# Values of dilated attention computed in token order and reordered through device memory

## The chip, the cores and the metric

The kernel runs on one core of one Trainium2 chip. Its time is what the device needs for one execution, in microseconds (us). TensorE multiplies matrices, VectorE and ScalarE work element by element, GpSimd helps, and SyncE (SP in the rows) issues the transfers between the device's memory (DRAM) and the on-chip memory (SBUF). Each engine takes its instructions in the order of the program and waits for semaphores; matmuls write to PSUM.

## The reference

Two transformer blocks, one behind the other, over 1024 tokens of width 1024, in 32-bit floats. The change concerns the first block's attention. Its 12 heads stand in three groups of four, with dilations 1, 4 and 16: in a group with dilation d a token sees those tokens before it that lie a multiple of d away.

```
ATT_GROUPS = ((128, 1), (512, 4), (2048, 16))      # window, dilation

def _dilated_window_attention(q, k, v, dilation, n_steps, slopes):
    def to_sub(t):
        t = t.reshape(B, L, dilation, H, Dh).transpose(0, 2, 1, 3, 4).reshape(Z, L, H, Dh)
    ...
    qb = to_sub(q).reshape(Z, nb, BLK, H, Dh).astype(jnp.float32)
    kb = band(to_sub(k)).astype(jnp.float32)
    vb = band(to_sub(v)).astype(jnp.float32)
    s = jnp.einsum('znqhd,znkhd->znhqk', qb, kb) * (Dh ** -0.5)
    ...
    s = jnp.where(valid[None, :, None], s + bias[None, None], -jnp.inf)
    lse = jax.nn.logsumexp(s, axis=-1)
    p = jnp.exp(s - lse[..., None])
    o = jnp.einsum('znhqk,znkhd->znqhd', p, vb)

def first_block(x, ...):
    u = _rmsnorm(h, norm_mix_g[l])
    z = jnp.einsum('bsd,dn->bsn', u, w_in[l])
    q, k, v, pz, ga, gp = jnp.split(z, offs, axis=-1)
    a = _attention_branch(q, k, v).astype(dt)
    ...
```

`to_sub` is the dilated order: all tokens with the same remainder modulo d stand together.

## The kernel before

The activations lie transposed in SBUF: channels on the 128 partitions, the 1024 tokens along the row. Every 32-bit product is made of three matmuls of the type fp32r: each operand is split into a high and a low part (`uh`, `ul` for the activations, `whi`, `wlo` for the weights), and high times high, high times low and low times high are summed. The division by the norm of a token (`rstd`) is done after the matmul, at the eviction from PSUM.

The program is a list of jobs, run in order by `run`. A job is one slab of weights (a `Unit`, 512 KB) and the matmuls that use it. Ahead of each job `run` emits the split of the next job's weights (ScalarE for `whi`, line 337, VectorE for `wlo`, line 338) and the load of weights for later jobs (line 320, on SP's queue), as far as the three `raw` buffers go. Attention is not a job: it is a chain of small steps (`attn1`, a generator in a lane of `bg`), and `tick`, called after every few matmuls of a job, advances it by one. A step (one block of 128 queries and two heads) consists of the scores (line 722), the softmax (VectorE line 737, which adds the table `alibi`, and ScalarE line 742), the flip (line 752, transposes on TensorE, copied back by lines 754 and 755) and the values (line 768). The table is loaded by line 705 when the chain first advances, and the result goes to DRAM by line 781.

For each group g there are jobs for two halves of q, two halves of k, and then one V job (`v_job`, lines 667 to 686) with two units. The V job makes the values with tokens on the partitions: here the activations are the stationary operand, 128 tokens at a time, and the weights (256 columns) the moving one. There are 2 halves x 4 blocks of tokens x 8 chunks of channels x 3 parts = 192 matmuls, lines 680 to 682. The block of tokens is picked by `tok`, in the order of the group: consecutive tokens for g = 0, every 4th for g = 1, every 8th for g = 2 (dilation 16 is treated as 8 with a mask). Since tokens stand on the partitions, `rstd` is needed as a column per block of tokens: `rcols`, ahead of the V job of group 0, transposes it for all three groups, 24 transposes with 6 small copies out of PSUM into `rcol`. `v_store1` scales and evicts each half of the values (line 694), into tiles that `attn1` reads from SBUF.

After the V job of group 1 come pool jobs, q and k of group 2, more pool jobs, the V job of group 2, and then the jobs `grp_job` and `pool_out_job`. The second block has two V jobs of its own in token order; their store (`v_store2`, line 1549) already goes through DRAM, and `attn2` loads windows of it (line 1563).

Of the kernel before, what the change touches and what calls it, by code (L numbers as in the profile page):

```python
# [10 lines left out]
F32 = mybir.dt.float32  # L11
F32R = mybir.dt.float32r
AF = mybir.ActivationFunctionType
ALU = mybir.AluOpType

P = 128
T = 1024
# [6 lines left out]
DIL = (1, 4, 16)  # L24
# [36 lines left out]
class Unit:  # L61


    def __init__(self, name, k0, kc, c0, cw):
        self.name, self.k0, self.kc, self.c0, self.cw = name, k0, kc, c0, cw
        self.n = kc * cw
        self.off = None
        self.early = 2
        self.parts = [self]
        self.raw = self.hi = self.lo = None  # L70
# [126 lines left out]
class Kern:  # L197
    def __init__(self, tc, ins, out, es):
        self.tc, self.nc, self.ins, self.out = tc, tc.nc, ins, out
        nc = self.nc  # L200
        self.pc = es.enter_context(tc.tile_pool(name="pc", bufs=1))
        self.pw = es.enter_context(tc.tile_pool(name="pw", bufs=3))
        self.pz = es.enter_context(tc.tile_pool(name="pz", bufs=36))
        self.pd = es.enter_context(tc.tile_pool(name="pd", bufs=1, space=bass.MemoryType.DRAM))
        self.pm = es.enter_context(tc.tile_pool(name="pm", bufs=2, space=bass.MemoryType.PSUM))
        self.pb = es.enter_context(tc.tile_pool(name="pb", bufs=4, space=bass.MemoryType.PSUM))
        self.bg = [deque(), deque(), deque()]
        self.late = []
        self.hook_wait = 0
        self.credit = 0.0  # L210
        self.rate = 0.0
        self.hooks = []
        self.ph = None
        self.phs = None

        self.cst = self.pc.tile([P, NCST], F32, tag="cst", name="cst")
        self.ones = self.pc.tile([P, P], F32R, tag="ones", name="ones")
        self.gg = self.pc.tile([P, 8], F32, tag="gg", name="gg")
        self.rcol = self.pc.tile([P, 24], F32, tag="rcol", name="rcol")
        self.cpos = self.pc.tile([P, 16], F32, tag="cpos", name="cpos")  # L220
        self.cneg = self.pc.tile([P, 16], F32, tag="cneg", name="cneg")
        self.oscr = [self.pd.tile([T, 264], F32, tag=f"oscr{g}", name=f"oscr{g}") for g in range(3)]
        self.v2 = [self.pd.tile([T, 256], F32, tag=f"v2{i}", name=f"v2{i}") for i in range(2)]
        self.x1 = [self.pd.tile([P, T], F32, tag=f"x1{i}", name=f"x1{i}") for i in range(NC)]
        self.sgr = [self.pd.tile([P, T], F32, tag=f"sgr{i}", name=f"sgr{i}") for i in range(NC)]
        self.sg2 = [self.pd.tile([P, T], F32, tag=f"sg2{i}", name=f"sg2{i}") for i in range(NC)]
        self.res = [self.pd.tile([P, T], F32, tag=f"res{i}", name=f"res{i}") for i in range(NC)]
        self.ud = [self.pd.tile([P, T], F32, tag=f"ud{i}", name=f"ud{i}") for i in range(NC)]
        self.po = [self.pd.tile([P, T], F32, tag=f"po{i}", name=f"po{i}") for i in range(NC)]
        self.hidd = [self.pd.tile([P, 2, T], F32, tag=f"hid{i}", name=f"hid{i}") for i in range(N_HID // 2)]  # L230
        self.quart = {(w, b, dp): {q: Quarter(w, b, dp, q) for q in ((0, 0), (0, 1), (1, 0), (1, 1))}
                      for w in ("w_mlp_out", "w_ff2") for b in range(N_BLK + 1) for dp in range(2)}
        self.sums = {(*key, i): self.pd.tile([P, T], F32, tag="sums" + "_".join(map(str, (*key, i))), name="sums")
                     for key in self.quart for i in (5, 6, 3, 7)}
        self.to_sum = list(self.quart)
        self.op = []
        self.nraw = 0
        self.rec = [self.pd.tile([P, T], F32, tag=f"rec{i}", name=f"rec{i}") for i in range(NC)]
# [357 lines left out]
                nc.sync.dma_start(y, x)  # L596
            yield

    def rcols(self, groups):
        nc = self.nc  # L600
        for g in groups:
            d = DIL[g]
            for q in range(2):
                ps = self.bank()
                for j in range(4):
                    nc.tensor.transpose(ps[:, j * P:(j + 1) * P], self.tok(self.rstd, d, 4 * q + j), self.ident())
                nc.vector.tensor_copy(
                    self.rcol[:, 8 * g + 4 * q:8 * g + 4 * q + 4],
                    ps.rearrange("p (j t) -> p j t", j=4)[:, :, 0],
                )  # L610

    @staticmethod
    def tok(ap, d, j):


        if d == 1:
            return ap[:, j * P:(j + 1) * P]
        if d == 4:
            return ap.rearrange("p (i d) -> p d i", d=4)[:, j // 2, (j % 2) * P:(j % 2 + 1) * P]
        return ap.rearrange("p (i d) -> p d i", d=8)[:, j, :]  # L620


    def qk_job(self, un, dst, d, scale, key):
# [40 lines left out]
                self.evac(lambda t=t, ps=ps: self.scaled(t, ps, 0.125))  # L664
        return fn

    def v_job(self, uns, store, d, g):

        nc = self.nc

        def fn():
            for q in range(2):
                ps = self.mm()
                for j in range(4):
                    o = ps[:, j * 256:(j + 1) * 256]
                    for k in range(NC):
                        un, kk = uns[k // 4], k % 4
                        uh, ul = self.us[k]
                        th, tl = self.tok(uh, d, 4 * q + j), self.tok(ul, d, 4 * q + j)
                        nc.tensor.matmul(o, th, un.h(kk, 0, 256), start=(k == 0), stop=False)  # L680
                        nc.tensor.matmul(o, th, un.l(kk, 0, 256), start=False, stop=False)
                        nc.tensor.matmul(o, tl, un.h(kk, 0, 256), start=False, stop=(k == NC - 1))  # L682
                        if k % 2 == 1:
                            self.tick()
                store(q, ps)
        return fn

    def v_store1(self, dst, g):
        nc = self.nc

        def store(q, ps):
            t = self.z(nm="v")
            for j in range(4):
                nc.vector.tensor_scalar(
                    t[:, j * 256:(j + 1) * 256], ps[:, j * 256:(j + 1) * 256],
                    self.rcol[:, 8 * g + 4 * q + j:8 * g + 4 * q + j + 1], None, ALU.mult,
                )
            dst["v", q] = t
        return store

    def attn1(self, g, src):
        nc = self.nc
# [1168 lines left out]
    def program(self):  # L1871
# [9 lines left out]
        qkv = [dict() for _ in range(3)]  # L1881
# [7 lines left out]
        for g in range(3):  # L1889
            pr.rate = RATE_A[g]  # L1890
            uns = [Unit("w_in", 0, NC, 256 * g + P * c, P) for c in range(2)]
            if g == 0:
                self.first = uns
                pr.job([], self.first_job(qkv[g]), 1)
            else:
                for c, un in enumerate(uns):
                    pr.job([un], self.qk_job(un, qkv[g], DIL[g], 0.125, ("q", c)))
            for c in range(2):
                un = Unit("w_in", 0, NC, 768 + 256 * g + P * c, P)
                pr.job([un], self.qk_job(un, qkv[g], DIL[g], None, ("k", c)), 1 if (g, c) == (0, 0) else None)  # L1900
            uns = [Unit("w_in", 4 * i, 4, 1536 + 256 * g, 256) for i in range(2)]
            vf = self.v_job(uns, self.v_store1(qkv[g], g), DIL[g], g)

            def vfn(vf=vf, g=g):
                if g == 0:
                    self.rcols(range(3))
                    self.phase("phA")
                vf()
                self.bg[0].append(self.attn1(g, qkv[g]))
                if g == 2:  # L1910
                    self.bg[0].append(self.combine1())
            if g == 2:
                pool_jobs((2, 1, 0))
            pr.job(uns, vfn)
            if g == 1:
                pool_jobs((5, 4, 3))
# [61 lines left out]
        for hh in range(2):  # L1978
# [6 lines left out]
                pr.job([un], self.qk2_job(un, qkv2[hh], ("k", c), None, 4 + 2 * hh + c),  # L1985
                       1 if (hh, c) == (0, 0) else None)
            uns = [Unit("w_in_2", 4 * i, 4, 1024 + 256 * hh, 256) for i in range(2)]
            vf = self.v_job(uns, self.v_store2(hh), 1, 0)

            def vfn2(vf=vf, hh=hh):  # L1990
                if hh == 0:
                    self.rcols((0,))
                    self.phase("phB")
                    self.bv = self.ph.tile([P, 512], F32, tag="bv", name="bv")
                    self.nc.sync.dma_start(self.bv, self.ins["bv"])
                    self.lru_const()
                vf()
                self.bg[0].append(self.attn2(hh, qkv2[hh]))
# [241 lines left out]
```

## Time and profile before

| | |
|---|---|
| median of three runs | 3020.59 us (3020.18 to 3021.07) |
| the profiled execution, its own time | 3018.67 us |
| its span in the trace | 3016.7 us |
| TensorE busy | 97% of the span |
| VectorE, ScalarE, GpSimd busy | 63%, 39%, 37% |

Times inside the trace are counted from the start of the span. The busy share is a mean over stages with different limits; what a change is worth is read in the stage that it touches.

### The profile page before, as it was taken

To read this page: it belongs to the slowest core of one execution; us is meant where nothing else is said; L and a number is where in the kernel's file an instruction comes from. 1 tells how busy PE (TensorE), PEld (TensorE's weight loads), DVE (VectorE), ACT (ScalarE), POOL (GpSimd) and SP (SyncE) were. 2 spreads that over 40 slices of the span, in tenths; PEclk is the share of its full clock that TensorE was granted. 3 is DMA by queue.
4 is the path that set the end of the run, shared out by engine and by line. 5 is a ranking of instruction groups with operands and counts; after the bars stand their busy time and mean duration, and the time that the engine had idled before them with its cause. 6 is when DMAs were issued, how large, how long until landed. Compare 5 with 4: busy or idle time off the path is not lost. (4 is left out here: it accounts for less than half of the span.)

```text
span 3016.7 us, 35237 instructions
## 1 busy us (share of the span) xinstructions
PE 2922.4 (97%) x13438; PEld 2406.6 (80%) x13438; DVE 1901.6 (63%) x2329; ACT 1168.6 (39%) x1786; POOL 1115.5 (37%) x554
## 2 busy tenths in 40 slices
PE   9999999999989999999899999998899899999987
PEld 8898987888878888877778778886788788888866
DVE  6424345565675567899844446888555765577797
ACT  3312044222344454334323325545424344444334
POOL 0012101555254433386400005544154444443486
PEclk9999999999999999999999999999999999999999
DMA  4201125778323355442232311211577233354442
GB/s 154 80 29 54 33 68 178 271 270 294 112 86 110 112 202 168 153 154 84 95 110 84 104 65 62 91 60 67 220 282 259 81 111 110 108 199 166 151 160 84
DMA packets 136567, 398.15 MB, mean 132 GB/s; under 512 B 14032, under 2 KB 29520, under 8 KB 136400
## 3 DMA queue, kind: packets, MB, share of 16 engines
q1 hardware_dynamic: 136400, 395.91, 37.7%
q8 instruction: 106, 1.74, 0.2%
q14 instruction: 61, 0.50, 0.1%
HBM read 285.66 MB, written 110.20 MB: 131 GB/s over the span
## 5 line engine op out<-in xcount | busy, mean ns | idle before, releaser
L1112 PE MATMUL bk<-obl,whi 128*128 128x512 f32 x864 | 340.9, 395 | 14.1 <-DVE obl L477 14.1
L1112 PE MATMUL bk<-obh,wlo 128*128 128x512 f32 x864 | 339.9, 393 | 1.5 <-DVE wlo L477 1.5
L476 ACT ACTIVATE whi<-raw 128x512 fp32r<-128x512 f32 (+2 forms) x256 | 204.7, 808 | 351.7 <-PE bk L1112 316.6
L1112 PE MATMUL bk<-obh,whi 128*128 128x512 f32 x864 | 339.6, 393 | 1.2 <-ACT obh L476 0.8
L477 DVE TENSOR_TENSOR wlo<-raw,whi 128x512 fp32r<-128x512 f32 (+2 forms) x256 | 306.2, 1199 | 50.2 <-ACT whi L476 48.7
L438 PE MATMUL mm<-uh,whi 128*128 128x512 f32 x864 | 278.0, 403 | 8.2 <-DVE v L1544 6.7
L1112 PE MATMUL bk<-tt,whi 128*128 128x512 f32 x896 | 275.7, 389 | 0.0
L438 PE MATMUL mm<-ul,whi 128*128 128x512 f32 x864 | 269.8, 393 | 2.2 <-DVE ul L490 2.2
L438 PE MATMUL mm<-uh,wlo 128*128 128x512 f32 x864 | 268.6, 392 | 0.1
L377 POOL TENSOR_TENSOR wsum<-wsum 128x1024 f32<-128x1024 f32 x64 | 180.2, 2825 | 238.4 <-DMA wsum<-in_w 227.3
L338 DVE TENSOR_TENSOR wlo<-raw,whi 128x1024 fp32r<-128x1024 f32 (+3 forms) x140 | 216.4, 1551 | 34.2 <-ACT whi L337 34.1
L477 DVE TENSOR_TENSOR obl<-hraw,obh 128x1024 fp32r<-128x1024 f32 x112 | 192.8, 1721 | 28.4 <-ACT obh L476 25.2
L438 PEld LDWEIGHTS mm<-uh,whi 128*128 128x128 f32 x864 | 157.2, 189 | 66.1 <-issue 34.2
L1112 PEld LDWEIGHTS bk<-obl,whi 128*128 128x128 f32 x864 | 164.3, 190 | 52.9 <-DVE obl L477 18.6
L337 ACT ACTIVATE whi<-raw 128x1024 fp32r<-128x1024 f32 (+3 forms) x140 | 135.3, 974 | 160.3 <-PE mm L682 94.0
L1112 PEld LDWEIGHTS bk<-tt,whi 128*128 128x128 f32 x896 | 168.2, 188 | 34.9
L438 PEld LDWEIGHTS mm<-ul,whi 128*128 128x128 f32 x864 | 163.4, 189 | 39.0 <-DVE ul L490 4.0
L1112 PEld LDWEIGHTS bk<-obh,whi 128*128 128x128 f32 x864 | 164.2, 190 | 36.5 <-ACT obh L476 1.2
L1112 PEld LDWEIGHTS bk<-obh,wlo 128*128 128x128 f32 x864 | 164.2, 190 | 36.3 <-DVE wlo L477 2.3
L438 PEld LDWEIGHTS mm<-uh,wlo 128*128 128x128 f32 x864 | 163.3, 189 | 35.5 <-DVE wlo L338 0.5
L1112 PE MATMUL bk<-tt,wlo 128*128 128x512 f32 x448 | 174.3, 389 | 0.0
L1731 POOL TENSOR_SCALAR yt<-yt 128x1024 f32<-128x1024 f32 x8 | 16.8, 2096 | 411.0 <-DMA sgr<-sgr 303.6
(362 smaller groups left out, 6510.3 us busy)
## 6 DMA issues: line engine op xcount, KB each, us to landing
raw<-in_w SPq DMA_DIRECT2D x190, 512.0 KB
wsum<-in_w SPq DMA_DIRECT2D x64, 512.0 KB
sums<-wsum SPq DMA_DIRECT2D x64, 512.0 KB
hraw<-hid SPq DMA_DIRECT2D x64, 512.0 KB
raw<-sums SPq DMA_DIRECT2D x64, 512.0 KB
hid<-h SPq DMA_DIRECT2D x56, 512.0 KB
wraw<-in_w SPq DMA_DIRECT2D x28, 512.0 KB
rb<-in_rpb SPq DMA_DIRECT2D x24, 384.0 KB
```

What stands on the lines that cost most here:

```text
L337: nc.scalar.activation(un.hi, un.raw, AF.Copy)
L338: nc.vector.tensor_tensor(un.lo, un.raw, f32(un.hi), ALU.subtract)
L377: G.tensor_tensor(d, x, y, f)
L438: nc.tensor.matmul(dst[a], w, half(x, a), start=(i == 0 and q == 0), stop=(i == n - 1 and q == 2),)
L476: self.nc.scalar.activation(hi, src, AF.Copy)
L477: self.nc.vector.tensor_tensor(lo, src, f32(hi), ALU.subtract)
L1112: nc.tensor.matmul(ps, w[:, k * P:(k + 1) * P], x, start=(k == 0 and q == 0), stop=(k == n - 1 and q == 2))
L1731: G.tensor_scalar(t, t, 0.044715, 1.0, ALU.mult, ALU.add)
```

## The change

The V jobs of groups 1 and 2 take their tokens in natural order, as group 0 does; `tok` and its strided views are gone. The evicted halves are stored to a DRAM tile (`v1`, one for each of the two groups), two stores of 512 KB. After the second half, `v_load` reads them back in the order that the attention wants: four transfers of 256 KB for group 1 (rows of 1 KB, every 4th token), two of 512 KB for group 2 (four rows of 1 KB that lie together, for each partition). The column of reciprocal norms is needed in one order only: `rcols` makes 8 transposes and 2 copies.

```
-        self.rcol = self.pc.tile([P, 24], F32, tag="rcol", name="rcol")
+        self.rcol = self.pc.tile([P, 8], F32, tag="rcol", name="rcol")
...
+        self.v1 = [self.pd.tile([T, 256], F32, tag=f"v1{i}", name=f"v1{i}") for i in range(2)]
...
-    def rcols(self, groups):
-        nc = self.nc
-        for g in groups:
-            d = DIL[g]
-            for q in range(2):
-                ps = self.bank()
-                for j in range(4):
-                    nc.tensor.transpose(ps[:, j * P:(j + 1) * P], self.tok(self.rstd, d, 4 * q + j), self.ident())
-                nc.vector.tensor_copy(
-                    self.rcol[:, 8 * g + 4 * q:8 * g + 4 * q + 4],
-                    ps.rearrange("p (j t) -> p j t", j=4)[:, :, 0],
-                )
+    def rcols(self):
+        nc = self.nc
+        for q in range(2):
+            ps = self.bank()
+            for j in range(4):
+                t = (4 * q + j) * P
+                nc.tensor.transpose(ps[:, j * P:(j + 1) * P], self.rstd[:, t:t + P], self.ident())
+            nc.vector.tensor_copy(
+                self.rcol[:, 4 * q:4 * q + 4], ps.rearrange("p (j t) -> p j t", j=4)[:, :, 0])
...
-                        th, tl = self.tok(uh, d, 4 * q + j), self.tok(ul, d, 4 * q + j)
+                        th, tl = (x[:, (4 * q + j) * P:(4 * q + j + 1) * P] for x in (uh, ul))
...
     def v_store1(self, dst, g):
         nc = self.nc
+        d = DIL[g]
 
         def store(q, ps):
             t = self.z(nm="v")
             for j in range(4):
                 nc.vector.tensor_scalar(
                     t[:, j * 256:(j + 1) * 256], ps[:, j * 256:(j + 1) * 256],
-                    self.rcol[:, 8 * g + 4 * q + j:8 * g + 4 * q + j + 1], None, ALU.mult,
+                    self.rcol[:, 4 * q + j:4 * q + j + 1], None, ALU.mult,
                 )
-            dst["v", q] = t
+            if d == 1:
+                dst["v", q] = t
+                return
+            v = self.v1[g - 1]
+            nc.sync.dma_start(
+                v[512 * q:512 * q + 512, :].rearrange("(j p) c -> p j c", p=P),
+                t.rearrange("p (j c) -> p j c", j=4))
+            if q == 1:
+                for r in range(2):
+                    dst["v", r] = self.v_load(v, d, r)
         return store
+
+    def v_load(self, v, d, q):
+
+        t = self.z(nm="vd")
+        o = t.rearrange("p (j c) -> p j c", j=4)
+        if d == 4:
+            src = v.rearrange("(h p d) c -> d p h c", p=P, d=4)
+            for e in range(2):
+                self.nc.sync.dma_start(o[:, 2 * e:2 * e + 2], src[2 * q + e])
+        else:
+            self.nc.sync.dma_start(o, v.rearrange("(p j) c -> p j c", j=8)[:, 4 * q:4 * q + 4])
+        return t
...
             def vfn(vf=vf, g=g):
                 if g == 0:
-                    self.rcols(range(3))
+                    self.rcols()
```

## Rows read from the trace of the kernel before

**Rows 1.** The page: the span, and busy time by engine.
```profile
span 3016.7 us, 35237 instructions
...
PE 2922.4 (97%) x13438; PEld 2406.6 (80%) x13438; DVE 1901.6 (63%) x2329; ACT 1168.6 (39%) x1786; POOL 1115.5 (37%) x554
```

**Rows 2.** By stretch: length, busy PE, PEld, DVE, ACT, POOL, granted clock, DMA share, GB/s.
```profile
138.00:203.00 65.00, 65.00 (x338) 61.85 (x338) 15.87 (x50) 11.69 (x35) 0.00 (x0) 1.00 0.11 35
```

**Rows 3.** Timeline of TensorE: start, duration, instruction; V jobs of groups 0, 1, 2.
```profile
56.49 0.36 PE L680 MATMUL mm<-whi,uh 128*128 128x256 f32 x1
...
79.59 0.63 PE L438 MATMUL mm<-uh,whi 128*128 128x512 f32 x2
...
189.05 0.40 PE L680 MATMUL mm<-whi,uh 128*128 128x256 f32 x1
...
201.65 0.63 PE L438 MATMUL mm<-uh,whi 128*128 128x512 f32 x2
...
338.03 0.29 PE L680 MATMUL mm<-whi,uh 128*128 128x256 f32 x1
...
384.13 0.62 PE L438 MATMUL mm<-plh,whi 128*128 128x512 f32 x2
```

**Rows 4.** Line 680's weight loads: shortest, median, longest (ns), first and last start.
```profile
L680 PEld LDWEIGHTS mm<-whi,uh x320: 186/192/341, 56.5 to 1643.1; 128*128 128x128 f32 x160
```

**Rows 5.** Timeline of TensorE: the 24 transposes of `rcols`.
```profile
53.07 2.06 PE L606 MATMUL bk<-cst,rstd 128*128 128x128 f32 x16
55.58 1.16 PE L606 MATMUL bk<-cst,rstd 128*128 128x128 f32 x8 [0.45 <-DVE rcol L607]
```

**Rows 6.** Timeline of SP's queue: at group 1's V job, and in block two.
```profile
185.72 0.42 SPq L320 DMA_DIRECT2D raw<-in_w  x1
186.19 0.44 SPq L705 DMA_DIRECT2D alibi<-in_alibi  x1
...
1645.42 0.38 SPq L1549 DMA_DIRECT2D v<-v  x1
...
1648.79 0.32 SPq L1563 DMA_DIRECT2D vw<-v  x1
```

**Rows 7.** Timeline of all engines after the V jobs of groups 1 and 2.
```profile
201.85 1.66 DVE L694 TENSOR_SCALAR v<-mm,rcol 128x256 f32<-128x256 f32 x4 [16.57 <-PE mm L682]
...
205.01 0.29 DVE L737 CUSTOM_DVE_ANT_0 s<-bk,alibi 128x128 f32<-128x128 f32 x1 [0.36 <-PE bk L722]
...
213.85 0.38 PE L752 MATMUL bk<-cst,s 128*128 128x128 f32 x2
...
227.36 1.04 ACT L337 ACTIVATE whi<-raw 128x1024 fp32r<-128x1024 f32 x1
...
391.51 0.28 DVE L737 CUSTOM_DVE_ANT_0 s<-bk,alibi 128x128 f32<-128x128 f32 x1
...
392.39 0.71 PE L752 MATMUL bk<-cst,s 128*128 128x128 f32 x2
...
396.52 0.56 PE L768 MATMUL bk<-v,pt 128*128 128x64 f32 x4
```

**Rows 8.** A 512 KB load and its reader (timeline); transfers from 75 to 79 us.
```profile
506.15 0.42 SPq L943 DMA_DIRECT2D uraw<-ud  x1
...
509.76 1.06 ACT L476 ACTIVATE ubh<-uraw 128x1024 fp32r<-128x1024 f32 x1 [2.30 <-DMA uraw<-ud]
...
DMA packets 358, 1.33 MB, mean 333 GB/s; under 512 B 33, under 2 KB 33, under 8 KB 358
```

**Rows 9.** TensorE after idle time (in brackets); one stretch with its granted clock.
```profile
505.04 1.22 PE L438 MATMUL mm<-ath,whi 128*128 128x512 f32 x2 [4.25 <-ACT merged L956]
...
505.00:510.00 5.00, 4.96 (x12) 3.90 (x13) 2.39 (x4) 2.70 (x5) 0.00 (x0) 0.50 0.57 174
...
2131.95 1.22 PE L438 MATMUL mm<-ah,whi 128*128 128x512 f32 x2 [2.71 <-DVE mixed L1843]
...
2148.51 0.73 PE L438 MATMUL mm<-ah,whi 128*128 128x512 f32 x2 [1.86 <-DVE mixed L1843]
```

More of the change, by code (lines that the diff above doesn't have):

```diff
@@ L597, in keep_x1 @@
             yield
-    def rcols(self, groups):
+    def rcols(self):
         nc = self.nc
-        for g in groups:
-            d = DIL[g]
-            for q in range(2):
-                ps = self.bank()
-                for j in range(4):
-                    nc.tensor.transpose(ps[:, j * P:(j + 1) * P], self.tok(self.rstd, d, 4 * q + j), self.ident())
-                nc.vector.tensor_copy(
-                    self.rcol[:, 8 * g + 4 * q:8 * g + 4 * q + 4],
-                    ps.rearrange("p (j t) -> p j t", j=4)[:, :, 0],
-                )
[L612 to L620, printed above, removed]
+        for q in range(2):
[5 more added lines that the diff above has]
+                self.rcol[:, 4 * q:4 * q + 4], ps.rearrange("p (j t) -> p j t", j=4)[:, :, 0])
     def qk_job(self, un, dst, d, scale, key):
@@ L665, in first_job, with v_job @@
         return fn
-    def v_job(self, uns, store, d, g):
+    def v_job(self, uns, store):
         nc = self.nc
@@ L1901, in program @@
             uns = [Unit("w_in", 4 * i, 4, 1536 + 256 * g, 256) for i in range(2)]
-            vf = self.v_job(uns, self.v_store1(qkv[g], g), DIL[g], g)
+            vf = self.v_job(uns, self.v_store1(qkv[g], g))
             def vfn(vf=vf, g=g):
                 if g == 0:
-                    self.rcols(range(3))
+                    self.rcols()
                     self.phase("phA")
@@ L1987, in program @@
             uns = [Unit("w_in_2", 4 * i, 4, 1024 + 256 * hh, 256) for i in range(2)]
-            vf = self.v_job(uns, self.v_store2(hh), 1, 0)
+            vf = self.v_job(uns, self.v_store2(hh))
             def vfn2(vf=vf, hh=hh):
                 if hh == 0:
-                    self.rcols((0,))
+                    self.rcols()
                     self.phase("phB")
```

## Prediction

> **What bounds the kernel now.** I read the page first: the span is 3016.7 us and TensorE is busy for 97% of it [rows 1]. The reader should see a kernel whose length is the sum of its matmuls, so that a change is worth what it takes off TensorE's line plus or minus what it makes TensorE wait. Then I went to the stage that the change touches with the table by stretches: over the V job of group 1 TensorE is busy in all 65.00 us, VectorE in 15.87, ScalarE in 11.69, and the DMA engines have a share of 0.11 [rows 2]. Nothing else is near its limit there. The V job of group 2 looks the same in the timeline: one matmul behind the other. So what these jobs cost is their matmul pitch, and I read that next, in the order of time.
>
> The V job of group 0 takes tokens in natural order. It runs from 56.49 to 79.59, its 192 matmuls alone on TensorE: 23.10 us, 0.1203 us each [rows 3]. The V job of group 2 has the same 192 matmuls of the same shape, with the stationary operand picked every 8th token: 338.03 to 384.13, 46.10 us, 0.240 each [rows 3]. In group 1 (every 4th token) attention steps of group 0 stand between the matmuls, so I take the end, where none do: 54 matmuls from 189.05 to 201.65, 0.2333 each [rows 3]. What differs is the weight load: line 680's takes from 186 to 341 ns [rows 4]. Loading 128 weights with a step doubles the pitch of a 256-column matmul, and that is what the change removes.
>
> [...]
>
> **What is removed.** Group 1's V job: 192 x (0.2333 - 0.1203) = 21.7 us. Group 2's: 46.10 - 23.10 = 23.0 us. The reciprocal norms: 24 transposes become 8. Today the first transpose is at 53.07 and the V job starts at 56.49; the last eight, after a wait of 0.45 on a VectorE copy, take from 55.58 to 56.49, 0.91 us [rows 3, 5]. With eight alone and two PSUM copies no bank has to be waited for: 3.42 - 0.91 = 2.5 us. The column of reciprocal norms is first needed by the V job's eviction, so no reader waits for it. Removed: 47.2 us, all from a line on which TensorE never idles.
>
> **What is added on the way.** For each of groups 1 and 2: two stores of 512 KB, four (group 1) or two (group 2) loads of 1 MB in all, on SP's queue. The eviction by VectorE is the same four instructions per half. As bytes this is 4 MB where the DMA engines stand at 0.11 [rows 2]: free. As a chain it isn't. The loads wait for the second store, and SP issues in order, so what the program puts on SP after them waits too. That is, for group 1, the weight load now issued at 185.72 and the alibi table of the group at 186.19, both 15 us *before* the V job ends at 201.65 [rows 6]; for group 2 the alibi table comes directly behind.
>
> When they arrive, counted from the end E of the V job: VectorE starts the last eviction 0.20 after E and needs 1.66 [rows 7], so the store is issued at E+1.9. The nearest row to a store that a load waits for is block two's own V store: issued 1645.42, first load behind it 1648.79, 3.37 us [rows 6]. The loads start at E+5.3. A 512 KB load takes from issue 506.15 to its reader's start at 509.76, 3.61 us [rows 8]; a further 512 KB behind it adds 1.57 us at the best rate seen, 333 GB/s [rows 8]. Group 2's alibi is the third 512 KB: E+5.3+3.61+2x1.57 = E+12.0. Group 1's is the fourth, behind the weights: E+13.6.
>
> Who waits. VectorE's first softmax step reads the table and is in order; behind it stand the second softmax step, the copies of the transposed scores and the next PSUM evictions. TensorE is in order too and stops at the first flip (line 752).
> Group 1: softmax now at E+3.4, flip at E+12.2 [rows 7]. From softmax to flip group 2 takes 0.88, and there the flip's second transpose is 0.33 late (0.71 for the two, 0.38 in group 1) [rows 7]; between 0.88 and 1.2 I take 1.1. With the table at E+13.6 the flip comes at E+14.7: 2.5 us idle.
> Group 2: softmax at E+7.4, flip 0.88 later at E+8.3 [rows 7]. With E+12.0 it comes at E+12.9: 4.6 us idle.
> The values themselves land before the tables, at about E+10.5, and are first read at E+12.4 in group 2 [rows 7], which the stall moves to E+17: no second wait.
>
> [...]
>
> One smaller loss: in group 1's V job six attention steps of group 0 remain, one per about 17 V matmuls. Between a step's scores and its flip lie now 17 x 0.2333 = 4.0 us, then 17 x 0.1203 = 2.0. A 128-wide step needs 0.88 from softmax to flip [rows 7]; these are 256 wide, so up to twice that, 1.8. It is on the edge: nothing if it fits, up to 1 us a step if a weight split is in VectorE's way, so 0 to 6; I take 1, as VectorE is busy for a quarter of that stretch [rows 2].
>
> **Sum.** -47.2 + (2.5 + 2.5) + (4.6 + 2.5) + 1.0 = -34.1 us. The profiled execution itself took 3018.67 us, its span and 2.0 around it; less 34.1 that is 2984.6. The median of the runs shown is 3020.59, 1.9 higher, so **2986.5 us**.
>
> Bounds of the unknown part, the tables' arrival. At the early end all transfers overlap and land 3.61 after E+5.3, at E+8.9: group 1 loses nothing, group 2 1.5 and no clock; the change is worth 47.2 - 1.5 - 1 = 44.7, or 2976. At the late end each transfer takes its full 3.61 behind the one before: group 2 E+16.1, 8.7 idle; group 1 E+19.7, 8.6 idle; with both clock losses and 2 in the V job the loss is 24.3, the change is worth 22.9, or 2998. I take the value between them because the bandwidth row is of transfers queued one behind another, as here.
>
> **The rivals.**
> *The wait is hidden* (22%): tables and values land early and only the V jobs' gain shows, 2972 to 2981. For it: 9 us of cover at group 1's softmax. Against: group 2 has only 0.88 us between softmax and flip, so something must show.
> *The wait is longer* (17%): the 1 KB rows of store and loads run well below 333 GB/s, or the values come after the tables' stall and stop TensorE again. 2992 to 3000.
> *The step isn't what costs* (2%): the pitch in the V jobs stays and only the waits are new: 3020.6 - 2.5 + 13.1 = 3031.2, slower. Against it stands group 0's job at half the pitch with the same shapes. [...]
> *Weights come late* (4%): SP now holds the weight load of 185.72 until about E+7, 23 us later against E, landing near E+12. It is split at 227.36, E+25.7 [rows 7], so 14 us of slack are left. From a landing after E+25.7 on, each us late costs TensorE one; at 34 us beyond it the gain is gone, and further on the kernel is slower. I halve this case between no change and slower.
>
> **Chances.** Forecast, 2981 to 2992: 55%. With the rivals the range 2972 to 2997 leaves out the last two (6%) and the tails of the first two (about 6%). About 0.2% (6 us) is what a measurement of this kernel can tell from no change: faster 94%, within it 2%, slower 4%.
>
> **What the changed profile would show.** Right: no weight load of line 680 near 341 ns; both dilated V jobs at a pitch of 0.12; eight transposes ahead of group 0's V job; SP standing for about 3.4 us between the second store and the first load; a TensorE gap at the first flip of each dilated group, of 2 to 5 us, with a granted clock of 0.5 for some 5 us behind it. Wrong: a pitch that stays above 0.2, gaps at the value matmuls or on a weight split instead of at the flips, no gap at all, or idle time inside group 1's V job of more than a few us.

## Result, and the profile after

The changed kernel takes 2984.98 us (median of 4 runs, 2983.65 to 2985.90), the kernel before 3020.39 on the same chip: a ratio of 0.9884, 95% interval 0.9869 to 0.9898. It is faster by 35.4 us; 2986.5 was forecast, a gain of 34.1. The span of the profiled execution fell from 3016.7 [rows 1] to 2981.9.

The timeline of TensorE in the changed kernel, the V jobs of the groups 0, 1, 2 (now lines 668 to 670) with the eight transposes ahead of the first; columns are start, duration, engine, line, instruction:

```profile
53.98 1.04 PE L606 MATMUL bk<-cst,rstd 128*128 128x128 f32 x8
54.78 0.36 PE L668 MATMUL mm<-whi,uh 128*128 128x256 f32 x1
...
77.89 0.63 PE L439 MATMUL mm<-uh,whi 128*128 128x512 f32 x2
...
140.87 0.38 PE L668 MATMUL mm<-whi,uh 128*128 128x256 f32 x1
...
177.96 0.63 PE L439 MATMUL mm<-uh,whi 128*128 128x512 f32 x2
...
319.86 0.28 PE L668 MATMUL mm<-whi,uh 128*128 128x256 f32 x1
...
342.89 0.63 PE L439 MATMUL mm<-plh,whi 128*128 128x512 f32 x2
```

These answer to [rows 3, 5]. Group 2's V job takes 342.89 - 319.86 = 23.03 us, where it took 46.10, and equals group 0's (23.11). Group 1's takes 37.09 with its attention steps, where it took 59.08: from 142.57, its first matmul in the kernel before, to 201.65 [rows 3].

```profile
142.57 0.51 PE L680 MATMUL mm<-whi,uh 128*128 128x256 f32 x1
```

The transposes take 0.80 from the first to the V job's first matmul, where it was 3.42. The weight loads of the V jobs, by source line (shortest, median and longest in ns), which answer to [rows 4]:

```profile
L668 PEld LDWEIGHTS mm<-whi,uh x320: 186/192/196, 54.8 to 1607.6; 128*128 128x128 f32 x160
```

No load near 341 ns is left. Now what was added. SP's queue behind the V jobs of groups 1 and 2 in the changed kernel (timeline):

```profile
179.85 0.37 SPq L691 DMA_DIRECT2D v<-v  x1
182.65 2.25 SPq L706 DMA_DIRECT2D vd<-v  x4
184.94 0.47 SPq L321 DMA_DIRECT2D raw<-in_w  x1
185.45 0.43 SPq L715 DMA_DIRECT2D alibi<-in_alibi  x1
...
344.78 0.38 SPq L691 DMA_DIRECT2D v<-v  x1
...
347.74 0.81 SPq L708 DMA_DIRECT2D vd<-v  x2
348.65 0.38 SPq L321 DMA_DIRECT2D raw<-in_w  x1
...
349.07 0.43 SPq L715 DMA_DIRECT2D alibi<-in_alibi  x1
```

The loads start 2.80 and 2.96 us after the second store, and the alibi tables of both groups stand behind them and behind a weight load. In the kernel before, group 1's table was issued at 186.19, 15 us ahead of its V job's end [rows 6]; now it is issued 7.5 us behind it (185.45 against 177.96). Who waits for it, in the timeline of VectorE (softmax, line 747) and TensorE (flip, line 762, and values, line 778), idle time and releaser in brackets:

```profile
192.85 0.29 DVE L747 CUSTOM_DVE_ANT_0 s<-bk,alibi 128x128 f32<-128x128 f32 x1 [11.89 <-DMA alibi<-in_alibi]
...
193.73 0.86 PE L762 MATMUL bk<-cst,s 128*128 128x128 f32 x2 [3.41 <-ACT s L752]
...
200.86 0.56 PE L778 MATMUL bk<-vd,pt 128*128 128x64 f32 x4
...
355.10 0.29 DVE L747 CUSTOM_DVE_ANT_0 s<-bk,alibi 128x128 f32<-128x128 f32 x1 [4.75 <-DMA alibi<-in_alibi]
...
355.99 0.86 PE L762 MATMUL bk<-cst,s 128*128 128x128 f32 x2 [4.79 <-ACT s L752]
...
362.24 0.56 PE L778 MATMUL bk<-vd,pt 128*128 128x64 f32 x4
```

TensorE stands still for 3.41 and 4.79 us at the first flips. VectorE's releaser is the table's transfer. At the value matmuls no idle time is shown, and these two gaps are all that TensorE waited for between 140 and 365 us (its waits there: us in total, times, longest):

```profile
PE bk L762 <- ACT s L752: 8.2, 2, 4.8
```

And the stretches behind the gaps (length, busy times, then granted clock, DMA share, GB/s):

```profile
193.70:198.70 5.00, 4.97 (x16) 3.29 (x17) 3.32 (x9) 2.94 (x11) 2.14 (x2) 0.66 0.02 3
356.00:361.00 5.00, 5.00 (x14) 3.67 (x15) 2.03 (x8) 3.13 (x12) 0.00 (x0) 0.50 0.00 0
```

By the us, the granted clock is 0.50 from 357.00 to 361.00 and 1.00 from 362.00 on; behind group 1's gap it is 0.50 from 194.70 to 196.70, 0.72 over the next us and 1.00 from 197.70 on. So 0.66 over 5 us is 0.50 for a part of them.

To see what both cost, take the first value matmul as a mark and count from the V job's end. For group 1 in the kernel before it is this one:

```profile
219.27 0.56 PE L768 MATMUL bk<-v,pt 128*128 128x64 f32 x4
```

Group 1: 17.62 before (219.27 against 201.65), 22.90 now: 5.28 lost, of which 3.57 by the flip (12.20 before [rows 3, 7], 15.77 now) and 1.7 behind it, at the lower clock. Group 2: 12.39 before [rows 3, 7], 19.35 now: 6.96 lost, 4.84 by the flip and 2.1 behind it. The account: 2.6 (transposes) + 22.0 + 23.1 - 5.3 - 7.0 = 35.4 us, for a span that fell by 34.8. Where the 0.6 between them lies was not traced.

### The profile page after: what moved, and what is told of

Its sections match the earlier page's. It is cut to its first block, busy times and chain, and to the rows that moved or that the text cites. A ratio compares the mean times of both kernels' runs of the same rounds, so it can differ in the third digit from the quotient of the medians.

```text
span 2981.9 us, 35224 instructions
## 1 busy us (share of the span) xinstructions
PE 2874.7 (96%) x13422; PEld 2357.2 (79%) x13422; DVE 1916.4 (64%) x2325; ACT 1170.6 (39%) x1786; POOL 1116.5 (37%) x554
## 5 line engine op out<-in xcount | busy, mean ns | idle before, releaser
L478 DVE TENSOR_TENSOR wlo<-raw,whi 128x512 fp32r<-128x512 f32 (+2 forms) x256 | 305.6, 1196 | 48.5 <-ACT whi L477 48.5
L439 PEld LDWEIGHTS mm<-uh,wlo 128*128 128x128 f32 x864 | 162.9, 189 | 35.4 <-DVE wlo L339 0.5
```

Source lines behind the costliest of these rows:

```text
L439: nc.tensor.matmul(dst[a], w, half(x, a), start=(i == 0 and q == 0), stop=(i == n - 1 and q == 2),)
L478: self.nc.vector.tensor_tensor(lo, src, f32(hi), ALU.subtract)
```

## Experiments

Two theories stood against each other. Mine: the strided weight loads and the 16 transposes fewer (2.6 of it) gave some 47 us, and the late tables took 12 of them back. The rival: the trip through memory is hidden, and the V jobs simply gave 35.

**Natural order without the trip.** The attention of the dilated groups reads the values in token order, so in groups 1 and 2 it weights values of other tokens.

```
-            if d == 1:
+            if d >= 1:
                 dst["v", q] = t
                 return
```

> The changed kernel with the way through memory left out: the dilated groups' attention reads the evicted values as they are, in token order, so its output is not the reference's in groups 1 and 2. My theory (the strided weight loads cost 47 us, the waits for the alibi tables take 12 back): both TensorE gaps at the first flips gone, 3020.4 - 47.7 = 2973, between 2970 and 2976. Rival (the waits cost nothing and the V jobs gave only 35): 2985, as the changed kernel.

Measured: 2971.99 us against 3019.07, ratio 0.9843 (0.9826 to 0.9859), 47.1 us faster. There is no TensorE idle time at the first flips of groups 1 and 2 (TensorE's timeline):

```profile
190.01 0.38 PE L762 MATMUL bk<-cst,s 128*128 128x128 f32 x2
...
345.70 0.72 PE L762 MATMUL bk<-cst,s 128*128 128x128 f32 x2
```

That is my theory's number; the removed part alone is worth 47.

**The trip without the natural order.** The kernel before, with

```
-            dst["v", q] = t
+            if DIL[g] == 1:
+                dst["v", q] = t
+                return
+            v = self.v1[g - 1]
+            nc.sync.dma_start(
+                v[512 * q:512 * q + 512, :].rearrange("(j p) c -> p j c", p=P),
+                t.rearrange("p (j c) -> p j c", j=4))
+            if q == 1:
+                for r in range(2):
+                    dst["v", r] = self.v_load(v, DIL[g], r)
...
+        src = v.rearrange("(q j p) c -> q p j c", q=2, p=P)[q]
...
```

where `v_load` reads the rows back in the order in which they were stored: its first half from the first store alone, its second half from the second.

> The kernel before, dilated weight loads and 24 transposes kept, with the stores, the wait and the loads through memory added (stored and read back in the same order; group 2's loads have rows of 1 KB). My theory: only the new waits show, gaps of some 3 and 5 us at the first flips and half clock behind each, 3020.4 + 12 = 3032, between 3029 and 3036. Rival (the trip is hidden): 3020.

Measured: 3028.96 us against 3019.07, ratio 1.0032 (1.0020 to 1.0044): slower by 9.9 where 12 was expected; the time lies just below the range of 3029 to 3036. The two gaps stand where they were expected (TensorE's timeline, then two stretches behind the gaps):

```profile
216.77 0.71 PE L773 MATMUL bk<-cst,s 128*128 128x128 f32 x2 [1.79 <-ACT s L763]
...
400.80 0.86 PE L773 MATMUL bk<-cst,s 128*128 128x128 f32 x2 [5.10 <-ACT s L763]
...
216.70:221.70 5.00, 4.87 (x22) 3.58 (x23) 3.36 (x9) 2.94 (x12) 2.11 (x2) 1.00 0.00 0
400.80:405.80 5.00, 5.00 (x17) 3.65 (x18) 2.04 (x8) 3.15 (x12) 0.00 (x0) 0.66 0.02 3
```

Group 1's gap is shorter than the 3 us expected, and behind 1.79 us of idle time the clock stays at 1.00, so only group 2 paid at a lower clock (0.66). The rival expected 3020 and falls: the trip is not hidden.

But this is not quite the wait of the changed kernel. There both halves of the values need both stores; here the loads of the first half need only the first store, and they are issued right behind the second one. SP's queue at group 1's V job, which ends here at 202.62:

```profile
204.51 0.37 SPq L703 DMA_DIRECT2D v<-v  x1
204.99 3.65 SPq L717 DMA_DIRECT2D vd<-v  x4
...
209.19 0.43 SPq L726 DMA_DIRECT2D alibi<-in_alibi  x1
```

The first load comes 0.48 us after the store, where it was 2.80, and the table is issued 6.57 us behind the V job's end, where it was 7.49. So 0.9 of the 1.6 us by which group 1's first flip comes sooner than in the changed kernel (14.15 behind the V job's end against 15.77) is this earlier issue. The experiment shows that the trip costs time by itself; what the change's own wait costs is read from the two runs that follow.

**The tables ahead of the stores.** The same transfers and all of the reference's work; only the place of the two table loads on SP's queue differs.

```
+    def table(self, g):
+        t = self.z(nm="alibi")
+        self.nc.sync.dma_start(t, self.ins["alibi"][g])
+        return t
...
-        bias = self.z(nm="alibi")
-        nc.sync.dma_start(bias, self.ins["alibi"][g])
+        bias = self.bias.pop(g) if g in self.bias else self.table(g)
...
+                if g > 0:
+                    self.bias[g] = self.table(g)
                 vf()
```

> The changed kernel with the alibi tables of groups 1 and 2 loaded ahead of the V job, so ahead of its stores on SP's queue. My theory (the table is what is late, the values have time): no gap at the first flips, 2985 - 12 = 2973, between 2971 and 2977. Rival (the values are as late as the table, it only came last): the gaps move from the flips to the first value matmuls, 2980 to 2985. Second rival: the early table finds no free buffer before the V job and holds up SP's queue, 2985 or more.

Measured: 2970.53 us against 3019.07, ratio 0.9840 (0.9825 to 0.9854): 48.5 us faster than the kernel before, and faster than the changed kernel. SP and TensorE in its timeline, the tables' issues and then the first flips and values of both groups:

```profile
141.29 0.44 SPq L714 DMA_DIRECT2D alibi<-in_alibi  x1
...
313.22 0.33 SPq L714 DMA_DIRECT2D alibi<-in_alibi  x1
...
189.90 0.38 PE L767 MATMUL bk<-cst,s 128*128 128x128 f32 x2
...
195.31 0.56 PE L783 MATMUL bk<-vd,pt 128*128 128x64 f32 x4
...
345.59 0.71 PE L767 MATMUL bk<-cst,s 128*128 128x128 f32 x2
...
349.73 0.56 PE L783 MATMUL bk<-vd,pt 128*128 128x64 f32 x4
```

No row carries idle time. The V jobs end at 177.69 and 337.34, so the first values come 17.62 and 12.39 after them, as in the kernel before. So the values' own trip, store, wait and loads, is fully covered; what had cost time was the table that SP's order put behind it. Both rivals of this experiment fall. It is also as fast as the kernel without the trip (2971.99), within the runs' spread.

**Only group 2's table early.** As above, with `if g == 2:`.

> The changed kernel with only group 2's alibi table loaded ahead of its V job. If the two waits are separate and each costs its gap and what the clock loses behind it (group 1: 3.4 and 1.9, group 2: 4.8 and 2.2), group 1's gap stays at 3.4 and the time is 2985 - 7 = 2978, 2976 to 2980. Rival (removing one wait only lets the next take it): 2982 to 2985.

Measured: 2977.38 us against 3019.26, ratio 0.9859 (0.9844 to 0.9874); 2978 was expected. The two waits are separate: group 2's gap is gone, group 1's is still there. In the timeline, group 1's first flip and group 2's, then the stretch behind group 1's gap:

```profile
191.62 0.71 PE L767 MATMUL bk<-cst,s 128*128 128x128 f32 x2 [2.42 <-ACT s L757]
...
347.61 0.72 PE L767 MATMUL bk<-cst,s 128*128 128x128 f32 x2
...
191.60:196.60 5.00, 4.92 (x22) 3.67 (x23) 3.31 (x9) 2.94 (x11) 2.15 (x2) 1.00 0.01 3
```

It was 2.42 here, 1 us shorter than in the changed kernel though its transfers are the same and are issued in the same order, and the clock stayed at 1.00. So the 3.4 and 1.9 that I had put on group 1 did not show in this trace. There is one trace of each kernel; that the gap varies from one execution of a kernel to the next is likely, but not shown.

**What makes the strided load slow.** The kernel before, with group 1's V job at other steps; the attention of the group then reads values of other tokens.

```
         if d == 4:
-            return ap.rearrange("p (i d) -> p d i", d=4)[:, j // 2, (j % 2) * P:(j % 2 + 1) * P]
+            return ap.rearrange("p (i d) -> p d i", d=2)[:, j // 4, (j % 4) * P:(j % 4 + 1) * P]
```

> The kernel before, with group 1's V job taking every 2nd token in place of every 4th (its values then stand in another order than its attention wants, so the output is not the reference's there). If any step makes the weight load slow: pitch 0.233 as at step 4, 3020. If what costs is that no two neighbours lie within 16 bytes, step 2 still has two of them and the pitch is near 0.12: 3020.4 - 22 = 2999. A pitch between the two, 0.16 to 0.2, would say that the cost grows with the step: 3006 to 3014.

And for step 3:

```
         if d == 4:
-            return ap.rearrange("p (i d) -> p d i", d=4)[:, j // 2, (j % 2) * P:(j % 2 + 1) * P]
+            return ap[:, 80 * j:80 * j + 3 * (P - 1) + 1:3]
```

> The kernel before, with group 1's V job taking every 3rd token (from overlapping stretches, so its values are not those of the reference's). Step 2 ran at the pitch of step 1. If it is two elements within 16 bytes that make a load cheap, step 3 has them only in part of its lines: a pitch between 0.12 and 0.233, say 0.15 to 0.2, 3004 to 3014. If the bound is a step of up to 2 elements: 0.233, 3020. If every step below 16 bytes is free: 0.12, 2997.

Measured: step 2 takes 2995.42 us against 3019.07, ratio 0.9924 (0.9909 to 0.9939), step 3 takes 3006.38 against 3019.26, ratio 0.9959 (0.9945 to 0.9973). The pitch in TensorE's timeline of the first, over 8 matmuls:

```profile
143.50 0.28 PE L681 MATMUL mm<-wlo,uh 128*128 128x256 f32 x1
...
144.47 0.28 PE L680 MATMUL mm<-whi,uh 128*128 128x256 f32 x1
```

and of the second, over 27:

```profile
185.82 0.34 PE L682 MATMUL mm<-whi,ul 128*128 128x256 f32 x1
...
190.50 0.34 PE L682 MATMUL mm<-whi,ul 128*128 128x256 f32 x1
```

0.97 / 8 = 0.121 at step 2, as at step 1; 4.68 / 27 = 0.173 at step 3; 0.2333 at step 4 and 0.240 at step 8 [rows 3]. Of the three readings for step 2 the one with two elements within 16 bytes had the pitch that was measured, and step 3 falls between, as that reading expected. The two others for step 3 (free, or full price) fall. The pitches also give the times: 192 x (0.2333 - 0.121) = 21.6 and 192 x (0.2333 - 0.173) = 11.6 us less than at step 4, and 23.7 and 12.9 were measured, which agrees within the intervals.

That it is the weight load that grows can be read from its own rows, line 681 in stretches of group 1's V job (us busy, mean ns of one): step 4 in the kernel before, step 2, step 3.

```profile
L681 PEld LDWEIGHTS mm<-wlo,uh 128*128 128x128 f32 x9 | 3.0, 329 | 0.0
...
L681 PEld LDWEIGHTS mm<-wlo,uh 128*128 128x128 f32 x14 | 2.7, 195 | 0.0
...
L681 PEld LDWEIGHTS mm<-wlo,uh 128*128 128x128 f32 x22 | 5.7, 261 | 0.0
```

At step 1 it is 192 (median).

## Why the prediction was right, point by point

- *What bounds the stage.* Right: the time moved by what TensorE's line lost and by what it came to wait for. 47.2 us were put on the removed part; the windows give 2.6 + 22.0 + 23.1 = 47.7 and the kernel without the trip 47.1.
- *The transposes, 2.5.* 2.6.
- *The loss inside group 1's V job, 1.0.* It isn't there: no idle time, and the job gave 22.0, more than the 21.7 of the pitch alone, as the first matmul behind each attention step became shorter too (0.39 against 0.51). The 2.0 us between scores and flip were enough.
- *When the loads start, E+5.3.* E+4.69 and E+4.85: the store and the wait took 2.80 and 2.96 where block two's row gave 3.37.
- *What stands ahead of the tables.* Wrong for group 2: the table does not come directly behind the values' loads, a weight load stands between. It landed at E+12.2 against E+12.0 all the same, by luck: the loads had started 0.45 earlier, and from their start the four transfers took 7.4 us, where the rates of [rows 8] give 8.3 for four. For group 1 it was E+14.9 against E+13.6: from the start of the loads 10.2 us, where 8.3 was counted. With four loads in rows of 1 KB ahead, the transfers from 182.6 to 193 ran at a mean of 251 GB/s, below the 333 of [rows 8]; that the short rows are the reason is not shown.
- *The gaps.* 3.41 against 2.5 and 4.79 against 4.6, at the first flips, as said. They are the price: removing their cause gives 12.2 us of span (2981.9 to 2969.7), and 5.28 + 6.96 is 12.24, both with what the clock cost behind them. The medians give 13.1 (48.5 - 35.4).
- *The clock, 2.5 twice.* No run shows this term of the sum: it was my estimate, half of a stretch of 5.00 us at a granted clock of 0.50 [rows 9]. In its place the changed kernel shows 1.7 and 2.1, once the gaps are taken off; behind group 1's gap the clock of 0.50 held for a part of the 5 us only (0.66 over all of them). That the clock fell for group 1 at all was luck for the forecast: the 2.5 us of idle time expected there lies between 1.86 and 2.71 [rows 9], but the length of a gap does not settle it (last section), and behind a gap of 2.42 in the kernel with only group 2's table early it did not fall.
- *The values land before they are read.* Right: no wait at lines 778 or 783, early table or late.
- *The rivals.* The late weights did not occur; nothing waited on a weight split. The longer wait occurred in one part, group 1's slower transfers, and was worth about 1 us; the values never stopped TensorE. The hidden wait is what the early table makes of the change. The 3031.2 of the case in which the step costs nothing has the 1.0 of the shorter pitch in it, which that case could not lose; without it, it is 3030.2.

The misses were of opposite signs: 0.5 too little removed, 1.0 too much inside the V job, 1.3 too little in the gaps (8.4 by the flips against 7.1) and 1.2 too much on the clock. The mechanism was right; that the total is nearer than its terms is luck.

## What to carry to other kernels

When a stationary operand is picked with a step, read the matmul pitch of that job against a job of the same shape without a step before anything else; a whole job at about twice its pitch shows in no idle time (here 0.2333 against 0.1203 us, and TensorE busy in all of the 65.00 us of group 1's stretch [rows 2, 3]). When a wait on an in-order queue is added, list what the program puts on that queue afterwards: here the new transfers had time enough, and a table that had nothing to do with them became late (group 1's was issued 7.5 us behind its V job's end, where it had been 15 ahead). Moving the table's two loads ahead of the waits was worth another 12.2 us of span to a change that gave 34.8.

## What was not expected of the hardware

For 128 weights of 4 bytes per partition and 256 moving columns, a matmul's pitch is 0.120 us at step 1 [rows 3], 0.121 at step 2, 0.173 at step 3, 0.233 at step 4 and 0.240 at step 8 [rows 3]. The prediction lets any step double the pitch; steps 4 and 8 do, step 2 does not, and a price that simply grew with the step would not be nearly the same at 4 and at 8. These pitches go with how many elements lie together in 16 bytes. Counted in pieces of 16 bytes, the 128 weights of a partition lie in 32, 64, 96, 128 and 128 of them; from 64 pieces on, the pitches come to 1.8 to 1.9 ns a piece, an estimate from them, and at 32 the pitch stays at 0.120. That is a reading of five pitches; how the weights are fetched, and what bounds the pitch at 32 pieces, is not shown.

TensorE's clock after idle time: over the 5 us behind a gap of 1.79 us (the trip without the natural order) and one of 2.42 us (only group 2's table early) the granted clock was 1.00; behind gaps of 3.41 and 4.79 in the changed kernel it was 0.66 and 0.50, and behind one of 2.71 in the kernel before [rows 9] it was 0.50, from 2131.90 to 2136.90. But the length of the gap does not settle it. At one and the same place of the program, a matmul that waits for `mixed` on VectorE, the changed kernel and the kernel without the trip have gaps of 2.15 and 2.16 us (timeline, then the stretch behind; the changed kernel first):

```profile
2096.36 0.73 PE L439 MATMUL mm<-ah,whi 128*128 128x512 f32 x2 [2.15 <-DVE mixed L1853]
...
2096.30:2101.30 5.00, 4.94 (x22) 4.10 (x23) 4.86 (x5) 4.00 (x5) 0.00 (x0) 1.00 0.98 367
```

```profile
2084.51 1.22 PE L439 MATMUL mm<-ah,whi 128*128 128x512 f32 x2 [2.16 <-DVE mixed L1853]
...
2084.50:2089.50 5.00, 4.99 (x15) 4.01 (x16) 4.86 (x4) 3.94 (x5) 0.00 (x0) 0.67 0.96 363
```

The first went on at 1.00, with 0.73 us for two matmuls, the second at 0.67, with 1.22. What else decides is not shown here. Group 1's wait cost 1.7 us beyond itself in the changed kernel (a gap of 3.41), and behind its 2.42 with only group 2's table early the clock stayed at 1.00: a forecast should carry both.
